# Seven block products for seven pairs of chunks of the first feed-forward layer too

## The chip, the cores and the metric

One core of a Trainium2 chip runs the whole program. The metric is the device time of one execution in microseconds; the kernel before has a median of 2299.14 us over three runs (2298.02 to 2299.99).

## The reference, cut to what matters

Two layers over 1024 tokens of width 1024, in float32. The first mixes tokens by gated linear attention and stick-breaking attention, the second by a convolution module; each is followed by a gated feed-forward layer (FFN) of width 2816.

```python
def swiglu(h, wg, wu, wd):
    return (jax.nn.silu(h @ wg) * (h @ wu)) @ wd

for layer in range(DEPTH):
    hn = rms_norm(h, mix_norm[layer])
    mix = hybrid_mixer(...) if layer % 2 == 0 else conformer_conv(...)
    h = h + mix
    h = h + swiglu(rms_norm(h, ffn_norm[layer]), ffn_w_gate[layer], ffn_w_up[layer], ffn_w_down[layer])
```

The convolution module is: a pointwise product to 2048 columns, a gate, a causal depthwise convolution of 31 taps, a layer norm over channels, swish, and a pointwise product back.

## The kernel before, in words

Every float32 operand is split into a rounded high part and the rest (`split`, `parts`), and each product takes three matmuls, high x high, high x low and low x high (`mm3`, lines 204 to 206). Residuals `xres` lie with tokens on partitions, 8 tiles of 128 tokens; activations for the products lie transposed, `hh_*`/`hl_*`, one pair for each half of 512 tokens. The 2816 columns of an FFN are 22 chunks of 128. `ffn_steps` builds for one half a step per chunk (gate, up, silu, product, split) and per group of chunks two down steps, each adding into `xres` (line 228). A step is a pair of functions, one that loads and splits weights and one that computes; `run` calls the first one step ahead. The weights' low parts are computed on the engine `weight_engine` names: VectorE in the first and last stage, GpSimd in the middle one. `raw_p` holds 2 raw weight tiles, `ws_p` 8 split ones.

A planner orders the instructions of each engine by program order and a simulated timeline, as far as dependences and free buffers allow; steps wrapped in `first` get priority by 2000 places. `behind` adds a dependence that only orders.

The stages: (1) attention. Near its end the attention of the second half (`a1`, `g1`, `o1`) is interleaved with all 22 FFN chunks of the first half (`f0`, groups of two). (2) The convolution stage: the output projection of the second half, then the pointwise chunks of the first half (`p0`) and the FFN of the second half (`f01`, groups of four) with the taps of the first half (`c0`, on VectorE, sums in PSUM) between; the layer norm `ln0`; then the second half's convolution (`c1`, two chunks of it on ScalarE and GpSimd) with the second FFN of the first half (`f10`, 11 chunks). `f10` stores the first of its two block products per matrix in DRAM (`m1_d`). (3) Five block products per matrix for the pairs of chunks f and f+11 of the second FFN: with the stored ones and the second one of `f10` these are seven block products (Winograd's form: 2 column blocks x 2 halves of the inner dimension x 2 halves of the tokens) in place of eight. Sums of token blocks (`token_sums`, `token_sum1`, `token_sum4`) overwrite the activations of both halves, sums of weight blocks are made in `pair_weights`, `pair_products` multiplies, `pair_down` adds the down products.

## Time and profile before

| | us |
|---|---|
| median of three runs | 2299.14 |
| the profiled execution | 2301.31 |
| its span, first to last instruction | 2299.5 |
| TensorE busy / VectorE / ScalarE / GpSimd | 2242.1 / 1591.4 / 959.5 / 473.9 |

The profile is of one execution. Busy times of TensorE (PE) overcount, since matmuls are pipelined: the distance between two starts is the better measure. PEld is TensorE's load of weights, DVE is VectorE, ACT ScalarE, POOL GpSimd. In the windows the clock is TensorE's granted clock as a share of its full one.

### The profile page before, as it was taken

To read this page: it belongs to the slowest core of one execution; us is meant where nothing else is said; L and a number is where in the kernel's file an instruction comes from. 1 tells how busy PE (TensorE), PEld (TensorE's weight loads), DVE (VectorE), ACT (ScalarE), POOL (GpSimd) and SP (SyncE) were. 2 spreads that over 40 slices of the span, in tenths; PEclk is the share of its full clock that TensorE was granted. 3 is DMA by queue.
4 is the path that set the end of the run, shared out by engine and by line. 5 is a ranking of instruction groups with operands and counts; after the bars stand their busy time and mean duration, and the time that the engine had idled before them with its cause. 6 is when DMAs were issued, how large, how long until landed. Compare 5 with 4: busy or idle time off the path is not lost.

```text
span 2299.5 us, 28002 instructions
## 1 busy us (share of the span) xinstructions
PE 2242.1 (98%) x10602; PEld 1855.6 (81%) x10602; DVE 1591.4 (69%) x2600; ACT 959.5 (42%) x1596; POOL 473.9 (21%) x255
## 2 busy tenths in 40 slices
PE   7999999999999999999999999999998899999999
PEld 6788888788888888888888887878886688888887
DVE  6587764878788755466677653897646677787776
ACT  6465544655565434423222254556345222222221
POOL 0000000000000004444444445979432000000000
PEclk9999999999999999999999999999999899999999
DMA  6254554223332334233222222233422222223222
GB/s 208 95 159 139 180 180 143 84 90 104 126 118 94 124 108 137 92 93 109 92 92 92 84 92 91 92 102 138 136 83 82 81 83 89 64 93 100 65 87 92
DMA packets 219637, 247.98 MB, mean 108 GB/s; under 512 B 9669, under 2 KB 169520, under 8 KB 219502
## 3 DMA queue, kind: packets, MB, share of 16 engines
q1 hardware_dynamic: 219502, 246.19, 33.1%
q8 instruction: 83, 1.36, 0.2%
q14 instruction: 52, 0.43, 0.1%
HBM read 219.42 MB, written 26.74 MB: 107 GB/s over the span
## 4 chain that ended last, share of the span: by engine, by line
PE 91%; DVE 4%; ACT 2%; DMA 1%; issue 1%; POOLq 0%; SPq 0%; POOL 0%; DVEq 0%; ACTq 0%
PE po L204 9%; PE po L205 9%; PE po L206 9%; PE pu L204 5%; PE pu L206 5%; PE pu L205 4%; PE pg L204 4%; PE pg L205 4%; PE pg L206 4%; PE pp L204 2%; PE pp L205 2%; PE pp L206 2%; PE po L674 2%; PE wt L656 1%; PE ps3u L204 1%
## 5 line engine op out<-in xcount | busy, mean ns | idle before, releaser
L941 DVE SCALAR_TENSOR_TENSOR cs<-u,wd,cs 128x512 f32<-128x512 f32 x406 | 306.2, 754 | 11.1
L228 DVE TENSOR_TENSOR xr<-xr,po 128x512 f32<-128x512 f32 x224 | 153.1, 684 | 157.7 <-PE po L206 156.7
L90 POOL TENSOR_TENSOR wl_wo<-raw_wo,wh_wo 128x1024 fp32r<-128x1024 f32 x8 | 19.1, 2398 | 883.4 <-ACT wh_wo L89 883.4
L1178 DVE TENSOR_TENSOR xr<-xr,po 128x512 f32<-128x512 f32 x176 | 120.1, 684 | 100.1 <-PE po L206 99.9
L204 PE MATMUL po<-wh_d,a 128*128 128x512 f32 x440 | 174.8, 399 | 6.9 <-ACT a L89 3.6
L204 PE MATMUL pg<-hh_f,wh_g 128*128 128x512 f32 x440 | 173.8, 395 | 5.5 <-DVE s L273 3.6
L206 PE MATMUL po<-wh_d,a 128*128 128x512 f32 x440 | 173.5, 395 | 4.1 <-DVE a L90 4.1
L205 PE MATMUL pg<-hl_f,wh_g 128*128 128x512 f32 x440 | 174.1, 396 | 0.0
L205 PE MATMUL po<-wl_d,a 128*128 128x512 f32 x440 | 173.7, 395 | 0.0
L206 PE MATMUL pg<-hh_f,wl_g 128*128 128x512 f32 x440 | 173.1, 394 | 0.0
L205 PE MATMUL pu<-hl_f,wh_u 128*128 128x512 f32 x440 | 172.7, 393 | 0.0
L204 PE MATMUL pu<-hh_f,wh_u 128*128 128x512 f32 x440 | 172.7, 393 | 0.0
L206 PE MATMUL pu<-hh_f,wl_u 128*128 128x512 f32 x440 | 172.6, 392 | 0.0
L89 ACT CAST wh_g<-raw_g 128x1024 fp32r<-128x1024 f32 x55 | 57.9, 1053 | 161.9 <-PE po L205 105.3
L90 POOL TENSOR_TENSOR wl_d<-raw_d,wh_d 128x1024 fp32r<-128x1024 f32 (+1 forms) x34 | 83.7, 2466 | 121.3 <-ACT wh_d L89 121.3
L90 POOL TENSOR_TENSOR wl_g<-raw_g,wh_g 128x1024 fp32r<-128x1024 f32 x33 | 79.3, 2404 | 135.6 <-ACT wh_g L89 131.6
L89 ACT CAST wh_d<-raw_d 128x1024 fp32r<-128x1024 f32 (+1 forms) x56 | 58.1, 1037 | 116.4 <-PE pu L205 66.8
L204 PEld LDWEIGHTS po<-wh_d,a 128*128 128x128 f32 x440 | 83.6, 190 | 25.6 <-DVE xr L228 4.7
L204 PE MATMUL po<-wh_dp,ap 128*128 128x512 f32 x264 | 102.0, 392 | 2.1 <-DVE xr L1178 1.0
L204 PE MATMUL pp<-hh_c,wh_p 128*128 128x512 f32 x256 | 100.0, 396 | 3.7 <-ACT hh_c L92 2.4
L204 PEld LDWEIGHTS pg<-hh_f,wh_g 128*128 128x128 f32 x440 | 83.5, 190 | 23.2 <-DVE s L273 3.8
L205 PE MATMUL pp<-hl_c,wh_p 128*128 128x512 f32 x256 | 101.7, 397 | 0.0
(440 smaller groups left out, 6067.6 us busy)
## 6 DMA issues: line engine op xcount, KB each, us to landing
raw_g<-in_ffn_w_gate_dram SPq DMA_DIRECT2D x27, 1024.0 KB, 5.2
raw_u<-in_ffn_w_up_dram SPq DMA_DIRECT2D x27, 1024.0 KB, 5.3
raw_p<-in_cv_w_pw_dram SPq DMA_DIRECT2D x16, 1024.0 KB, 5.4
raw_d<-in_ffn_w_down_dram SPq DMA_DIRECT2D x14, 1024.0 KB, 4.9
raw_d<-in_ffn_w_down_dram SPq DMA_DIRECT2D x24, 512.0 KB, 3.5
raw_g<-in_ffn_w_gate_dram SPq DMA_DIRECT2D x23, 512.0 KB
raw_u<-in_ffn_w_up_dram SPq DMA_DIRECT2D x23, 512.0 KB
raw_dp<-in_ffn_w_down_dram SPq DMA_DIRECT2D x22, 512.0 KB, 3.7
```

Source lines behind the costliest of these rows:

```text
L89: nc.scalar.copy(hi, src)
L90: (eng or nc.vector).tensor_sub(lo, src, r32(hi))
L204: nc.tensor.matmul(ps, sh, mh, start=first, stop=False, **kw)
L205: nc.tensor.matmul(ps, sh, ml, start=False, stop=False, **kw)
L206: nc.tensor.matmul(ps, sl, mh, start=False, stop=last, **kw)
L228: nc.vector.tensor_add(xt[i][:, cs], xt[i][:, cs], po)
L656: nc.tensor.transpose(pt[:, col:col + P], wrow[bi][:, P * j:P * j + P], ident)
L674: nc.tensor.matmul(po[:, lo_c:256], st["v"][j // 4][:, j % 4, e, :], m[:, 256 * jj + lo_c:256 * jj + 256], start=(last and jj == 0 and m i ...
L941: i = nc.vector.scalar_tensor_tensor(out, tap, w, acc, op0=ALU.mult, op1=ALU.add)
L1178: nc.vector.tensor_add(xres[i][:, cs], xres[i][:, cs], po)
```

## The change

The first FFN gets the same treatment as the second, for 14 of its 22 chunks: pairs f and f+7, f from 0 to 6. Chunks 14 to 21 stay plain.

- The first half's FFN beside the attention shrinks to chunks 0 to 6 (with stored first products) and 14 to 18.
- A new stage follows: chunks 19 to 21 of the first half, the output projection of the second half between, the token sums, the last two downs, then five block products for seven pairs.
- The convolution stage starts behind it. The FFN of the second half in it is chunks 14 to 21 alone. Chunks 1 and 4 of the first half's convolution run on ScalarE and GpSimd, as chunks 1 and 4 of the second half's did.
- The second FFN's order changes: chunk 10 runs ahead of the last pointwise products, groups are 3, 2, 3 and 3 chunks, and the token sums are one function for both layers. It keeps the first sum in PSUM, scales on two engines, makes the low parts of three sums on GpSimd and overwrites the first half's blocks at once. `token_sum4` also takes its low part from GpSimd and is put behind the last but one step.
- PSUM pools are given per tag, buffers `ft` 3 in place of 4 in the convolution stage and 10 in place of 6 in the last.

```diff
-    def ffn_steps(l, h, hT, xt, ps, ft, act, use_silu, group, last=NF, early=None):
+    def ffn_steps(l, h, hT, xt, ps, ft, act, use_silu, groups, keep=None):
...
-        f0 = ffn_steps(0, 0, lambda: hf, xres, ps, ft, act, False, 2)
+        f0 = ffn_steps(0, 0, lambda: hf, xres, ps, ft, act, False,
+                       [[0, 1], [2, 3], [4, 5], [6], [14, 15], [16, 17], [18]], m1_d[0])
...
-            + a1[:2] + [ffn_in] + interleave(f0[:-12], interleave(a1[2:], g1 + o1)) + f0[-12:])
+            + a1[:2] + [ffn_in] + interleave(f0[:-4], interleave(a1[2:], g1 + o1)) + f0[-4:])
...
+    def token_sums(l, hi_lo, ps, tags, ft, tiles, t3=None):
...
+        for j in range(2):
+            for i in range(4):
+                BOTH[i % 2](xn[i][j], xt[i][:, 512 * j:512 * j + 512], rs[:, i:i + 1])
+        for k in range(4):
...
+            nc.scalar.mul(r2, pt[1], g2)
+            nc.scalar.mul(b22[0][k], pt[1], g2)
+            sub1(r3, pt[0], g1, r2)
+            if t3 is not None:
+                split(b12[0][k], b12[1][k], pt[0], g1)
+            sub1(pt[0], pt[0], g1, r32(b11[0][k]))
+            nc.vector.tensor_sub(r1, pt[0], r32(b11[1][k]))
+            sub1(r2, pt[1], g2, r1)
+            split(t2[0][k], t2[1][k], r2, eng=nc.gpsimd)
+            sub1(b22[1][k], pt[1], g2, r32(b22[0][k]))
+            for t, r in ((t3 or b12, r3), (b11, r1)):
+                split(t[0][k], t[1][k], r, eng=nc.gpsimd)
+        return (b11, t2, t3 or b12, b21, b22), hi_lo[1]
+
+    def five_products(l, blocks, es, order):
...
+        before_t4 = marks[-2]
+
+        def token_sum4(k):
...
+            i = nc.vector.tensor_add(r, r32(t4[0][k]), r32(t4[1][k]))
+            behind(i.ins, before_t4)
...
+            split(t4[0][k], t4[1][k], r, eng=nc.gpsimd)
...
+            if l == 0 and f == NP - 1:
+                late = [pair_down(f, (0, 1), (h,)) for h in range(2)]
+            else:
+                late = [pair_down(f, (j,), (0, 1)) for j in range(2)]
+        return steps, late
...
+    with ExitStack() as mid:
+        weight_engine[0] = nc.vector
...
+            ps = psum_pools(es, "ps0", (("b", 2), ("a", 4), ("n", 2)))
...
+            f0 = ffn_steps(0, 0, lambda: hf, xres, ps, ft, act, True, [[19, 20, 21]])
+            load_x(1)
+            run(f0[:2] + out_project(1, ps, ft) + f0[2:3])
...
+            blocks, hT["f01"] = token_sums(0, hf, ps, ("n", "a"), ft, xn, [[t3[:, m, k, :] for k in range(4)] for m in range(2)])
+            run(f0[3:])
+        with ExitStack() as es:
+            steps, late = five_products(0, blocks, es, (("act", 4), ("s", 4), ("ft", 6), ("w", 2)))
+            run(steps + late)
...
-        f01 = ffn_steps(0, 1, lambda: hT["f01"], xres, ps, ft, act, True, 4)
-        f10 = ffn_steps(1, 0, lambda: hT["f10"], xres, ps, ft, act, True, 4, NP, m1_d)
-        c0 = conv_steps(0, range(NK))
+        f01 = ffn_steps(0, 1, lambda: hT["f01"], xres, ps, ft, act, True, [[14, 15, 16, 17], [18, 19, 20, 21]])
+        f10 = ffn_steps(1, 0, lambda: hT["f10"], xres, ps, ft, act, True,
+                        [[0, 1, 2], [3, 4], [5, 6, 7], [8, 9, 10]], m1_d[1])
+        c0 = interleave(conv_steps(0, (0, 2, 3, 5, 6, 7)), conv_steps(0, (1, 4), (1, 4)))
...
-        run([norm_step(0, mixg[1], "c0"), lambda: add_bias(0)] + p0[:2] + [norm_step(1, ffng[0], "f01")]
-            + interleave(p0[2:] + f01[:25], c0) + interleave(f01[25:31], ln0) + f01[31:]
-            + [norm_step(1, mixg[1], "c1"), lambda: add_bias(1)] + q0[:1] + p1[:2]
-            + interleave(q0[1:2] + p1[2:4] + q0[2:], c1[0])
-            + [norm_step(0, ffng[1], "f10")] + interleave(p1[4:] + f10[:9], c1[1])
-            + interleave(f10[9:13], ln1) + pw2(1, s1) + [token_sums] + f10[13:15] + [token_sum1] + f10[15:])
...
+        run([norm_step(0, mixg[1], "c0"), lambda: add_bias(0)] + f01[:2] + p0[:2]
+            + interleave(p0[2:] + f01[2:9], c0) + interleave(f01[9:], ln0)
+            + [norm_step(1, mixg[1], "c1"), lambda: add_bias(1)] + q0[:2] + p1[:2]
+            + interleave(p1[2:4] + q0[2:], c1[0])
+            + [norm_step(0, ffng[1], "f10")] + interleave(p1[4:] + f10[:12], c1[1])
+            + interleave(f10[12:14] + f10[16:17], ln1) + pw2(1, s1))
+        xn = [t for pair in u_pairs("xn_f11") for t in pair]
+        blocks, _ = token_sums(1, hT["f10"], ps, ("n", "a"), ft, xn)
+        run(f10[14:16] + f10[17:])
```

## Rows read from the trace of the kernel before

**Rows 1.** Part 1 of the page: busy time and share of each engine.
```profile
PE 2242.1 (98%) x10602; PEld 1855.6 (81%) x10602; DVE 1591.4 (69%) x2600; ACT 959.5 (42%) x1596; POOL 473.9 (21%) x255
```
**Rows 2.** Timeline of TensorE, last stage: start, duration, instruction.
```profile
1817.72 0.39 PE L205 MATMUL ps2g<-hl_f,wh_s3ag 128*128 128x512 f32 x1
...
1819.98 0.39 PE L206 MATMUL ps1u<-t,wl_s24u 128*128 128x512 f32 x1
```
**Rows 3.** Windows: busy us (instructions) of PE, PEld, DVE, ACT, POOL; clock, DMA.
```profile
430.00:800.00 370.00, 366.14 (x1883) 306.71 (x1882) 294.18 (x444) 198.81 (x377) 0.00 (x0) 1.00 0.33 104
...
960.00:1310.00 350.00, 350.00 (x1561) 289.72 (x1560) 237.01 (x328) 94.19 (x113) 154.71 (x77) 1.00 0.30 97
...
1394.00:1435.00 41.00, 37.27 (x171) 29.85 (x170) 14.45 (x30) 21.19 (x36) 20.07 (x14) 0.96 0.15 55
1435.00:1650.00 215.00, 211.15 (x943) 174.25 (x942) 179.55 (x249) 114.56 (x169) 167.26 (x103) 0.99 0.34 112
...
1741.00:1811.30 70.30, 50.55 (x201) 39.10 (x199) 55.89 (x89) 30.41 (x49) 16.53 (x6) 0.81 0.28 86
1811.30:2299.50 488.20, 482.30 (x2112) 394.72 (x2112) 357.43 (x517) 112.84 (x150) 0.00 (x0) 1.00 0.26 84
```
**Rows 4.** Timeline of TensorE, transition of the second FFN.
```profile
1760.79 1.03 PE L1032 MATMUL pt_f<-ident,xn_f 128*128 128x128 f32 x8
...
1773.11 0.63 PE L205 MATMUL pg<-hl_f,wh_g 128*128 128x512 f32 x1
1773.54 0.63 PE L206 MATMUL pg<-hh_f,wl_g 128*128 128x512 f32 x1
```
**Rows 5.** Groups of VectorE instructions, 430 to 800 us: busy, mean ns, idle before.
```profile
L228 DVE TENSOR_TENSOR xr<-xr,po 128x512 f32<-128x512 f32 x56 | 38.1, 681 | 13.0 <-PE po L206 12.9
L90 DVE TENSOR_TENSOR wl_u<-raw_u,wh_u 128x1024 fp32r<-128x1024 f32 x17 | 20.7, 1219 | 0.8 <-ACT wh_u L89 0.8
...
L273 DVE TENSOR_TENSOR s<-s,pg 128x512 f32<-128x512 f32 x18 | 12.3, 681 | 0.1
```
**Rows 6.** Timeline of VectorE, transition of the second FFN.
```profile
1740.98 0.69 DVE L228 TENSOR_TENSOR xr<-xr,po 128x512 f32<-128x512 f32 x1 [2.03 <-PE po L206]
...
1748.59 0.16 DVE L112 SCALAR_TENSOR_TENSOR rs_f<-nt_f,rs_f 128x4 f32<-128x4 f32 x1
...
1753.68 0.75 DVE L1039 SCALAR_TENSOR_TENSOR r<-pt_f,vb,hh_f 128x512 f32<-128x512 f32 x1 [1.37 <-PE pt_f L1032]
...
1762.82 0.74 DVE L1041 SCALAR_TENSOR_TENSOR r<-pt_f,vb,r 128x512 f32<-128x512 f32 x1
1763.48 0.74 DVE L93 SCALAR_TENSOR_TENSOR hl_f<-pt_f,vb,hh_f 128x512 fp32r<-128x512 f32 x1
...
1793.81 1.27 DVE L228 TENSOR_TENSOR xr<-xr,po 128x512 f32<-128x512 f32 x2
```
**Rows 7.** Groups of GpSimd instructions, 1441 to 1606 us.
```profile
L935 POOL TENSOR_TENSOR cv<-cv,tap 128x512 f32<-128x512 f32 x60 | 77.8, 1296 | 7.2 <-ACT tap L934 4.7
L90 POOL TENSOR_TENSOR wl_p<-raw_p,wh_p 128x1024 fp32r<-128x1024 f32 x11 | 26.5, 2405 | 9.9 <-ACT wh_p L89 9.9
```
**Rows 8.** Timeline of VectorE, convolution of the first half.
```profile
1086.30 4.71 DVE L941 SCALAR_TENSOR_TENSOR cs<-u,wd,cs 128x512 f32<-128x512 f32 x6
```
**Rows 9.** Timeline of VectorE, layer norm statistics of one tile.
```profile
1347.90 1.29 DVE L961 BATCH_NORM_STATS2 bst<-plt 128x6 f32<-128x512 f32 x2 [5.54 <-PE plt L960]
...
1353.97 0.16 DVE L965 SCALAR_TENSOR_TENSOR lv<-lv 128x1 f32<-128x1 f32 x1
```
**Rows 10.** Timeline of GpSimd (POOL) and VectorE (DVE), the same transition.
```profile
1743.69 2.40 POOL L90 TENSOR_TENSOR wl_u<-raw_u,wh_u 128x1024 fp32r<-128x1024 f32 x1
1743.79 2.32 DVE L105 TENSOR_SCALAR nv_f<-s_f 128x4 f32<-128x4 f32 x1
...
1778.53 6.29 POOL L90 TENSOR_TENSOR wl_d<-raw_d,wh_d 128x1024 fp32r<-128x1024 f32 x1 [19.85 <-ACT wh_d L89]
1783.13 2.23 DVE L1110 TENSOR_TENSOR raw_g<-s1g,raw_g 128x512 f32<-128x512 f32 x1
```

More of the change, by code (lines that the diff above doesn't have):

```diff
@@ L26 @@
 NF = DFF // P
-NP = NF // 2
+NPS = (7, NF // 2)
 EPS = 1e-6
@@ L251, in chunk @@
                 pr.append(ps.tile([P, 512], F32, name=f"p{t}{nm}", tag="a"))
-                if early is None:
+                if not kept:
                     for k in range(NK):
@@ L255, in chunk @@
                             k == 0, k == NK - 1)
-            if early is not None:
+            if kept:
                 for k0 in (0, 4):
@@ L330, in trunk @@
     o_d = dr("o_d", [8, P, T])
-    m1_d = dr("m1_d", [2, NP, P, TH])
+    m1_d = [dr(f"m1_d{l}", [2, NPS[l], P, TH]) for l in range(2)]
     xres = [None] * NT
@@ L1084, in token_sum4 @@
-        def token_sum4(k):
-            r = ft(f"t4_{k}")
-            nc.vector.tensor_add(r, r32(t4[0][k]), r32(t4[1][k]))
-            nc.vector.tensor_sub(r, r, r32(t2[0][k]))
-            nc.vector.tensor_sub(r, r, r32(t2[1][k]))
-            split(t4[0][k], t4[1][k], r)
-        def product(pm, w, b, first=True, alone=False):
-            for k in range(4):
-                mm3(pm, w[0][:, k, :], w[1][:, k, :], b[0][k], b[1][k], first and k == 0, k == 3,
-                    skip_group_check=not alone)
```

304 lines of the change are left out of this document (151 added, 153 removed).

## The prediction, made before the changed kernel was run

> **What bounds the kernel now.** I read the page's busy times first: TensorE is busy 98% of the span, VectorE 69% [rows 1]. Since matmuls overlap, busy is not the measure; the start-to-start pitch is. In the last stage ten pitches of 512 columns take 2.26 us, so one costs 0.2267 us [rows 2]. The table by stage comes next [rows 3]: 430 to 800 us (first FFN of the first half, with the attention of the second half), 960 to 1310 (first FFN of the second half with the convolution of the first) and the last stage keep TensorE at 99 to 100%. Work taken from TensorE is therefore time, as long as nothing else comes late in its place. One stretch is different: from the last residual add that the second half's norm needs, at 1741.0 us, to the first of the five block products at 1811.3 us. It holds 169 matmuls of 512 columns and 32 transposes (201 in all), 169 x 0.227 + 32 x 0.11 (8 transposes take 1.03 us end to end [rows 4]) = 41.8 us of work at the full clock, in 70.3 us: 28.5 us are lost there (granted clock 0.81; after an idle spell the pitch is 0.43 us, the 1.2 GHz level [rows 4]). VectorE is busy 55.9 of the 70.3 us. This stretch is the model for the new one that the change builds in the first FFN.
>
> **What is removed.** Seven pairs of chunks, gate and up each, take seven block products in place of eight. A block product is 4 x 3 = 12 matmuls, so 7 x 2 x 12 = 168 matmuls go: 168 x 0.2267 = **38.1 us** of TensorE. Transposes (32 for the norm of the second half) and the down products keep their number. This is the only gain that is certain; all else is where TensorE will wait.
>
> **Attention of the second half (430 to 800).** The filler shrinks from 18 chunks and 14 downs of two chunks to 12 chunks, 8 such downs and 2 of one chunk. TensorE loses 6 x 48 + 120 = 408 matmuls = 92 us of the 370; 277 are left. VectorE loses per chunk two weight splits of 1.22 and three passes of 0.68 (4.5 us, x 6 = 27), and 16 adds of 0.68 and 7 weight splits of 1.22 (19 us) [rows 5]: 294 - 46 = 248 us [rows 3]. It would be 89% full, against 80% now with 3.9 us of TensorE idle, and against 84% with 3.9 us idle in 1435 to 1650 [rows 3]. I take **+3 us** (bounds 0 and 15). The copies and stores of the kept first products (14 of each) lie on ScalarE, busy 199 of 370 us, and on the DMA engines, busy a third [rows 3]; nothing.
>
> **New stage, its token sums.** T0 is the last add of the output projection of the second half. Today's case shows the chain behind such an add: the root is done 7.8 us later, the first token sum starts after 12.7 us [rows 6]. The change splits the scaling between two engines; I take 10.5. On VectorE then stand 24 passes (6 per k) at a pitch of 0.66 = 15.8, 16 adds of the last two downs at 0.60 = 9.6 [rows 6], product and split of chunk 21, 1.2, one down weight split 1.2 and one of the first pair's weights, 1.2: 29 us. At a fill of 85% (80% in today's stretch [rows 3]) that is 34 us: the first product starts at T0 + 44.6. TensorE has from T0 on chunk 21 and the two downs, 48 + 72 matmuls, and 32 transposes: 30.7 us. Lost: 14 us. The fourth token sum then must be there within four products (10.9 us): 12 passes, 7.2 us, and its GpSimd halves take 1.3 us each [rows 7]. Its first pass is pinned behind the last but one down; product five waits for it, and the sums for the up matrix's weights stand behind it in VectorE's queue: +2. **+16 us**, bounds: 0, if TensorE finds filler as it does in nearly all of 960 to 1310, and 28.5, today's whole loss.
>
> **The same stretch in the second FFN** is rebuilt. Chunk 10 moves ahead, so that the halves can be overwritten at once, and the cover is four downs of 36 matmuls and 32 transposes, 36.2 us. VectorE: 20 passes 13.2, 28 adds 16.8, weight sums 2.4, one split 1.2: 33.6, at 85% 39.5 us, so T0 + 50: 14 lost. The fourth sum is pinned in the same way, and its GpSimd halves (4 x 1.3) compete with down weights of 2.4 us: +5. 19 in place of 28.5: **-10 us** (bounds -25 and +5).
>
> **Convolution stage.** 14 of 22 chunks of the second half leave it, and with them 228 us of cover; out-projection and one norm leave too. Chunks 1 and 4 of the first half's convolution go to ScalarE and GpSimd. VectorE keeps 6 x 31 = 186 taps. They depend on one another: six take 4.71 us, 0.785 each [rows 8], 146 us; some 34 other passes between them cost about 0.5 each where they fill that latency: 17. From its start TensorE has 6 pointwise and 6 FFN chunks and 4 downs of 48 matmuls, 768 x 0.2267 = 174 us, and 64 transposes, 7. The convolution ends at 163; behind it four layer norm statistics of some 4 us (6.2 in the row, 2.2 of it blocked [rows 9]) and half the swish, 22 us in all: 185 against 181. Then +4, and +2 for queueing; the second norm behind it gets two downs as cover in place of one and returns the 3.7 us idle of 1394 to 1435 [rows 3]. **+2 us** (bounds -5 and 30). GpSimd carries 60 adds of 1.30 and weight splits of 2.40 [rows 7], some 150 us in these 163; in 1435 to 1650 it was busy 167 of 215 with TensorE idle 3.9 [rows 3]. The second half's convolution has the same taps and about the same cover: **+1** (bounds -4 and 8). The second layer norm keeps 3 chunks as cover and loses a down of 48 matmuls, 10.9 us: **+3** (0 and 11).
>
> **Stage changes.** Attention to the new stage: 38 us of cover (four downs, two chunks) where 87 stood. Five products to convolution: the last pair's halves are ordered so that 48 matmuls of downs and two chunks (33 us) lie over the norm, but the last activation is not covered. **+4** (0 and 10). DMA and SP's queue: 14 more stores and loads of 256 KB, and the loads of x moved ahead, at a DMA share of a quarter to a third [rows 3]; nothing. Five products in steady state ran 488 us with 5.9 idle [rows 3], most of it at the end of the kernel; 7 pairs the same: nothing.
>
> **A rule against the change.** The first token sums and all of the fourth put 16 splits on GpSimd. Today a VectorE pass over 4 columns takes 2.32 us while GpSimd runs a split (others of the kind 0.16 [rows 6]), a GpSimd split takes 6.29 in place of 2.40 beside VectorE's passes, and a VectorE pass 2.23 behind it [rows 10]. The Trainium skill (SBUF — State Buffer, "Who interferes with whom") states that a VectorE instruction with two SBUF inputs and a GpSimd instruction that reads SBUF exclude each other for a whole instruction; the trace agrees with these rows. By that rule the token sums, with one input in PSUM, run free, but the fourth one does not; with it the sum is the third rival's, without it the +2 and +5 above stand.
>
> **Sum.** -38.1 + 3 + 16 - 10 + 2 + 1 + 3 + 4 = -19.1 us. The profiled execution took 2301.3 us (span 2299.5 and 1.8 around it): 2282.2. The median of the runs, 2299.14, lies 2.2 below it: **2280**.
>
> **Rivals.**
> 1. Less is lost: the planner finds filler, and the new stretch costs no more than a us or two, as 960 to 1310 shows for a well filled stage. -19.1 - 14.3 = -33: 2266. Against it: VectorE's queue of 29 us stands whatever TensorE does.
> 2. No change: the new stretch costs today's full 28.5 us and the old one stays. -38.1 + 3 + 28.5 + 2 + 1 + 3 + 4 = +3.4: 2302.5. For it: the same dependences, and less cover than today (30.7 against 41.8 us).
> 3. Slower, by the shared port: each of the four GpSimd splits of the fourth sum takes 6.29 in place of 2.40, and product five waits: 4 x 3.9 = 15.6 at each of both places, -19.1 + 31.2 = +12: 2311. It decides once one such split delays TensorE by more than 2.4 us. Against it: the other products and adds from PSUM open gaps.
> 4. Slower, by the convolution: TensorE doesn't run ahead, so it follows VectorE (163 against 141 us up to the last FFN chunk of that stage, 22) and then has too little cover for the statistics (13 more): 35 in place of 2 on that term, 2313. It decides once TensorE idles over 21 us more in that stage. Against it: today the passes of the FFN slip between the taps.
> That the change doesn't do what it says would show as more than 10,434 matmuls, and I give it nothing.
>
> **Chances.** Forecast 0.54 (own range 2262 to 2294), rival 1 0.13, rival 2 0.12, rival 3 0.11, rival 4 0.10. A measurement can tell about 0.2% (4.6 us) from no change: faster 0.67, same 0.12, slower 0.21. The range reaches from below rival 1 to just short of rival 3: 2258 to 2310.
>
> **What would show it.** About 10,434 TensorE instructions on the page (records can be missing); a stretch between the last add of the output projection and the first block product of the first FFN with some 16 us lost and the clock below 1; the second such stretch shorter than 70 us; VectorE near 90% beside the attention of the second half and in the convolution of the first; GpSimd splits well over 1.3 us in the stretches (rival 3). I am wrong if the new stretch loses under 5 or over 25 us, or if TensorE idles over 10 us in the convolution of the first half.

## The result, and the profile after

The changed kernel takes **2387.9 us** in the median of 4 runs (2386.95 to 2388.62) beside 2299.56 of the kernel before on the same chip: **1.0383 times** as long, 95% interval 1.0365 to 1.0401. Forecast were 2280, range 2258 to 2310. The profiled execution has a span of 2385.2 us; the clock granted over the whole of it is 0.97.

The page's first part, busy time and share of each engine, against [rows 1]:

```profile
PE 2240.0 (94%) x10434; PEld 1843.5 (77%) x10434; DVE 1697.1 (71%) x2784; ACT 1003.7 (42%) x1684; POOL 476.5 (20%) x299
```

The 168 matmuls are gone (10602 to 10434). TensorE's busy time is nearly what it was, 2240 against 2242, although 38 us of work went: a matmul takes longer where the granted clock is low, and that is 0.97 over the span where it was 0.99. VectorE is busy 106 us more. The windows of the changed kernel, in the columns of [rows 3], cut at events (last output of an attention unit 763.5; last add of the output projection 836.6; first block product 887.9; statistics of the norm ahead of the convolution 1224.8; first chunk of pointwise products through 1257.6; first layer norm statistics 1447.5; then the second half's convolution, layer norm and token sums):

```profile
430.00:763.50 333.50, 308.91 (x1554) 255.71 (x1552) 266.96 (x416) 186.37 (x369) 0.00 (x0) 0.95 0.35 112
763.50:836.60 73.10, 72.49 (x317) 59.45 (x318) 31.91 (x40) 26.41 (x41) 0.00 (x0) 1.00 0.29 95
836.60:887.90 51.30, 25.74 (x124) 20.02 (x123) 49.05 (x81) 25.06 (x41) 20.96 (x14) 0.81 0.24 72
887.90:1224.80 336.90, 327.71 (x1425) 267.40 (x1426) 225.48 (x325) 83.85 (x119) 20.93 (x13) 0.99 0.26 83
1224.80:1257.60 32.80, 29.46 (x131) 23.34 (x131) 11.18 (x28) 16.13 (x23) 14.50 (x11) 0.92 0.11 35
1257.60:1447.50 189.90, 182.34 (x798) 149.82 (x797) 162.56 (x224) 87.25 (x117) 160.67 (x103) 0.99 0.31 100
1447.50:1487.70 40.20, 21.98 (x93) 17.87 (x94) 20.79 (x85) 20.60 (x40) 0.50 (x3) 0.60 0.04 13
...
1580.40:1758.60 178.20, 173.78 (x775) 142.90 (x774) 142.59 (x200) 90.07 (x129) 124.80 (x76) 0.98 0.37 118
1758.60:1809.70 51.10, 39.30 (x182) 32.01 (x181) 25.72 (x82) 24.22 (x37) 11.51 (x5) 0.83 0.26 91
...
1844.00:1893.80 49.80, 35.88 (x174) 29.36 (x172) 41.44 (x75) 21.63 (x37) 29.18 (x19) 0.92 0.22 69
1893.80:2382.10 488.30, 484.91 (x2112) 396.08 (x2112) 364.23 (x520) 115.70 (x153) 6.72 (x4) 0.99 0.27 86
```

As in the prediction, **lost** is the elapsed time less TensorE's work in it (0.2267 us for each matmul of 512 columns, fewer columns in proportion, 0.11 for a transpose). It holds idle time and the low clock together. Between the same events of both kernels:

| stretch | lost before | lost after | more | forecast |
|---|---|---|---|---|
| up to 430 us | 43.5 | 43.1 | -0.4 | 0 |
| 430 to the last attention unit | 12.8 | 50.8 | +38.0 | +3 |
| output projection | (stage changes) 2.1 | 1.2 | -0.9 | |
| first FFN's token sums, to the first product | - | 27.2 | +27.2 | +16 |
| five products of the first FFN, norm ahead of the convolution | - | 22.3 | +22.3 | +4 |
| first half's convolution and layer norm | 0.5 | 35.8 | +35.3 | +2 |
| up to the second half's layer norm | 12.5 | 11.7 | -0.8 | +1 |
| second half's layer norm | 2.6 | 16.9 | +14.3 | +3 |
| second FFN's token sums | 28.9 | 14.5 | -14.4 | -10 |
| last stage | 6.3 | 9.6 | +3.3 | 0 |

The last stage is counted up to its last add to the residual, some 3 us ahead of the span's end in both kernels. The sum of "more" is +123.9 us; less the 38.1 saved it is +85.8, the difference of the two spans (2385.2 - 2299.5 = 85.7).

What such a stretch looks like: TensorE's timeline at the first half's layer norm; in brackets the idle time ahead of an instruction and what ended it.

```profile
1446.21 0.47 PE L1161 MATMUL plt<-ident,cv 128*128 128x128 f32 x1 [6.19 <-DVE cv L1142]
1451.04 1.97 PE L1161 MATMUL plt<-ident,cv 128*128 128x128 f32 x8 [4.35 <-ACT lx L1168]
1457.41 1.97 PE L1161 MATMUL plt<-ident,cv 128*128 128x128 f32 x8 [4.41 <-ACT lx L1168]
1463.86 1.97 PE L1161 MATMUL plt<-ident,cv 128*128 128x128 f32 x8 [4.49 <-ACT lx L1168]
1470.31 1.97 PE L1175 MATMUL pls<-ident,lx 128*128 128x128 f32 x8 [4.48 <-ACT lx L1168]
```

The four tiles of statistics follow one another 6.4 us apart with nothing between them, and eight transposes take 1.97 us where they took 1.03 [rows 4]: the granted clock is 0.60 there. The chain is that of [rows 9]; before, the chunks of the first FFN lay over it.

### The profile page after: what moved, and what is told of

Same layout as the page of the kernel before. It is cut to its first block, busy times and chain, and to the rows that moved or that the text cites. A ratio compares the mean times of both kernels' runs of the same rounds, so it can differ in the third digit from the quotient of the medians.

```text
span 2385.2 us, 28069 instructions
## 1 busy us (share of the span) xinstructions
PE 2240.0 (94%) x10434; PEld 1843.5 (77%) x10434; DVE 1697.1 (71%) x2784; ACT 1003.7 (42%) x1684; POOL 476.5 (20%) x299
## 4 chain that ended last, share of the span: by engine, by line
PE 83%; DVE 10%; ACT 2%; DMA 2%; issue 1%; SPq 0%; DVEq 0%; ACTq 0%
PE po L205 8%; PE po L206 8%; PE po L207 8%; PE pg L205 3%; PE pg L207 3%; PE pg L206 2%; PE pu L205 2%; PE pu L207 2%; PE pu L206 2%; PE pp L205 2%; PE pp L206 2%; PE pp L207 2%; PE ps3u L205 1%; PE ps3u L206 1%; PE ps2u L207 1%; PE ps2u L206 1%
## 5 line engine op out<-in xcount | busy, mean ns | idle before, releaser
L205 PE MATMUL po<-wh_dp,ap 128*128 128x512 f32 x432 | 167.1, 392 | 3.8 <-DVE xr L1015 2.1
L207 PE MATMUL po<-wh_dp,ap 128*128 128x512 f32 x432 | 165.3, 390 | 0.9 <-DVE ap L91 0.9
L206 PE MATMUL po<-wl_dp,ap 128*128 128x512 f32 x432 | 165.9, 389 | 0.0
L1136 POOL TENSOR_TENSOR cv<-cv,tap 128x512 f32<-128x512 f32 x120 | 155.6, 1296 | 11.2 <-ACT tap L1135 4.9
L205 PE MATMUL po<-wh_d,a 128*128 128x512 f32 x272 | 109.1, 402 | 7.8 <-DVE xr L229 7.8
L205 PE MATMUL pg<-hh_f,wh_g 128*128 128x512 f32 x272 | 107.7, 397 | 5.5 <-DVE s L277 4.6
L207 PE MATMUL po<-wh_d,a 128*128 128x512 f32 x272 | 107.8, 398 | 0.2 <-DVE a L91 0.2
L206 PE MATMUL pg<-hl_f,wh_g 128*128 128x512 f32 x272 | 107.6, 395 | 0.0
L206 PE MATMUL po<-wl_d,a 128*128 128x512 f32 x272 | 107.2, 394 | 0.0
L207 PE MATMUL pu<-hh_f,wl_u 128*128 128x512 f32 x272 | 107.1, 394 | 0.0
L207 PE MATMUL pg<-hh_f,wl_g 128*128 128x512 f32 x272 | 106.9, 393 | 0.0
L1135 ACT ACTIVATE tap<-u,wd 128x512 f32<-128x512 f32 x120 | 84.6, 720 | 50.9 <-POOL cv L1136 50.8
```

Of the source, the lines that this page charges most:

```text
L205: nc.tensor.matmul(ps, sh, mh, start=first, stop=False, **kw)
L206: nc.tensor.matmul(ps, sh, ml, start=False, stop=False, **kw)
L207: nc.tensor.matmul(ps, sl, mh, start=False, stop=last, **kw)
L1135: nc.scalar.mul(m, tap, w)
L1136: nc.gpsimd.tensor_add(acc, acc, m)
```

## The experiments

The theory at the start: TensorE's chunks, moved out of the attention and convolution stages, had been cover for the chains of other engines. Rivals: GpSimd's splits hold VectorE up; the second FFN's rebuild is the cause; the work is there but TensorE's planned order puts it in the wrong place; another engine's total work sets a stage's length.

### Which part of the change: l1_only, l0_only

Edit of l1_only (layer 0 and the convolution of the first half as before):

```diff
-        f0 = ffn_steps(0, 0, ..., [[0, 1], [2, 3], [4, 5], [6], [14, 15], [16, 17], [18]], m1_d[0])
+        f0 = ffn_steps(0, 0, ..., [[f, f + 1] for f in range(0, NF, 2)])
...
-    with ExitStack() as mid:
...
```

> The second FFN's part of the change alone (its token sums, its order of chunks, its fourth sum pinned); the first FFN and the first half's convolution as before. Cover theory (TensorE's other work, moved out of the attention and convolution stages of the first FFN, leaves chains bare there): the stretch in front of the second FFN's products loses some 14 us in place of 28.7, the second layer norm some 8 to 16 in place of 2.7, so 2286 to 2300 us, faster than before or the same. If the loss of the changed kernel sat mainly in the second FFN's rebuild, this would be slower than before by over 30 us. Port theory (GpSimd's splits of the token sums hold VectorE up): the stretch in front of the products does not shrink, 28 us or more lost, and the time is 2300 or above.

Edit of l0_only: the second FFN's token sums, its order and its last stage are the ones of before.

```diff
-        blocks, _ = token_sums(1, hT["f10"], ps, ("n", "a"), ft, xn)
-        run(f10[14:16] + f10[17:])
+            + interleave(f10[9:13], ln1) + pw2(1, s1) + [token_sums] + f10[13:15] + [token_sum1] + f10[15:])
```

> The first FFN's part alone (seven pairs, the stage of its own, convolution behind it with two chunks on ScalarE and GpSimd); the second FFN as before. Cover theory: attention tail 36 us lost, token sums 27, norm ahead of the convolution 15, first layer norm 33, against 38 saved: 2385 to 2400 us, the whole of the loss and a little more, since the second FFN's transition again loses about 28. If the two parts disturb one another, this is well below 2380.

Measured: l1_only 2304.1 us, ratio 1.0019 (1.0010 to 1.0028); l0_only 2387.5, ratio 1.0384 (1.0369 to 1.0400). The first FFN's part carries the whole loss. The second FFN's part is worth nothing, as a sum of large terms: the stretch of its token sums loses 12.5 us in place of 28.9, but the layer norm ahead of it 15.7 in place of 2.6 and the last stage 12.5 in place of 6.3. The stretches of l1_only: convolution and layer norm of the second half, token sums, last stage:

```profile
1498.80:1675.50 176.70, 172.82 (x773) 141.89 (x772) 133.33 (x188) 87.30 (x125) 120.88 (x73) 0.99 0.38 120
1675.50:1725.40 49.90, 38.09 (x182) 31.16 (x181) 25.71 (x82) 24.12 (x37) 11.54 (x5) 0.86 0.28 92
1759.70:1807.40 47.70, 38.55 (x173) 30.04 (x172) 43.12 (x69) 20.80 (x34) 27.73 (x18) 0.96 0.31 95
1807.40:2298.70 491.30, 484.68 (x2113) 395.50 (x2111) 366.77 (x526) 116.77 (x155) 7.38 (x4) 1.00 0.26 83
```

### The size of the shift: np4, att_cover, att_less

```diff
# np4 (of the lists of chunks, the ends of the lines)
-NPS = (7, NF // 2)
+NPS = (4, NF // 2)
-[[0, 1], [2, 3], [4, 5], [6], [14, 15], [16, 17], [18]], m1_d[0])
+[[0, 1], [2, 3], [8, 9], [10, 11], [12, 13], [14, 15], [16, 17], [18]], m1_d[0])
-[[14, 15, 16, 17], [18, 19, 20, 21]])
+[[8, 9, 10, 11], [12, 13, 14, 15], [16, 17, 18, 19], [20, 21]])
# att_cover (the end of a line, and the stage behind)
-[16, 17], [18]], m1_d[0])
+[16, 17], [18, 19], [20]], m1_d[0])
-            f0 = ffn_steps(0, 0, lambda: hf, xres, ps, ft, act, True, [[19, 20, 21]])
+            f0 = ffn_steps(0, 0, lambda: hf, xres, ps, ft, act, True, [[21]])
...
# att_less (the end of a line)
-[[0, 1], [2, 3], [4, 5], [6], [14, 15], [16, 17], [18]], m1_d[0])
+[[0, 1], [2, 3], [4, 5], [6]], m1_d[0])
```

> Four pairs in place of seven: TensorE saves 21.8 us in place of 38.1, three more chunks and their downs (49 us of work) lie beside the attention, six more chunks (98 us with their downs) beside the convolution. Cover theory: the attention tail loses under 10 us in place of 36, the first layer norm under 10 in place of 33, the token sums and the norm ahead of the convolution still 27 and 15: 38.1 - 21.8 - 28 - 25 = -37, some 2350 us, less if the norms find more cover. Theory that the pairs themselves or their stores and loads cost time, pair by pair: 88 us x 4/7 = 50 above before, also near 2350; they part in where it goes: by the second the attention stage and the layer norm keep more than half their losses. Theory that it is the new stage as such (its barriers and transitions, whatever the number of pairs): the saving falls and the loss stays, 2404 us.

> Chunks 19 and 20 and their downs, 144 matmuls or 33 us of work, go from the new stage into the attention stage; nothing else is changed. Cover theory with a tail that only lacks cover: the attention stage ends at the same time (763 us) with 33 us of work more in it, its tail loses 36 - 33 = 3 to 8 us; the token sums lose as much more as they lose cover (two downs of one chunk in place of three: 11 us) and the output projection loses the two chunks beside it: net -10 to -22, some 2365 to 2378. Cover as a zero-sum game between the two places: no change, 2388. If the attention's tail is slow for another reason (VectorE full, GpSimd, DMA), its end moves back by the 33 us of added work and the time rises, 2395 or more.

> The changed kernel without chunks 14 to 18 of the first half and their downs (360 matmuls, 81.6 us of TensorE's work, left out); VectorE loses some 45 of its 266 us with them, ScalarE some 15. Floor theory (the attention's own chain takes some 330 us whatever lies beside it, as att_hold's 328 suggests): the attention ends at 755 to 764 as before, and of the 81.6 us nearly all is lost: 2365 to 2378. VectorE theory: 221 us of work at the same 80% fill take 276, the stage ends near 710, 2325 to 2340. TensorE theory (units at the tail's bare pace of 12 us as soon as nothing lies beside them): it ends near 680, below 2310.

Measured: np4 2340.1 us, ratio 1.0176 (1.0159 to 1.0193); att_cover 2391.7, ratio 1.0402 (1.0387 to 1.0418); att_less 2348.7 in one run.

With four pairs the convolution and its layer norm lose 1.1 us in place of 35.8: there the work was cover, and enough of it covers all. The token sums (27.6) and the norm ahead of the convolution (21.3) lose with four pairs what they lose with seven. The stretches of np4: attention, token sums, convolution, layer norm:

```profile
430.00:785.40 355.40, 344.04 (x1772) 287.84 (x1770) 288.45 (x441) 195.90 (x377) 0.00 (x0) 0.99 0.36 112
860.40:912.10 51.70, 25.98 (x124) 19.92 (x123) 49.02 (x82) 24.98 (x41) 20.92 (x14) 0.80 0.24 71
1150.30:1364.40 214.10, 214.10 (x950) 177.16 (x949) 166.41 (x229) 95.48 (x128) 170.23 (x108) 1.00 0.30 98
1364.40:1428.50 64.10, 63.48 (x309) 52.84 (x307) 37.28 (x91) 30.65 (x44) 28.63 (x12) 1.00 0.27 95
```

The attention stage still loses 23.5, though 49 us of work came back to it; in att_cover, with 35 us more work, it ends 22 us later. So its tail does not simply lack work. (What att_cover won there, 13 us, the output projection and the token sums lost again, which had given up the work.) These are the attention stages of before, after and the kernels that differ in its work, from 430 us to the last unit:

| kernel | TensorE's work, us | length, us | VectorE busy, us | its fill (busy share) |
|---|---|---|---|---|
| before | 356 | 369.2 | 294 | 80% |
| att_cover | 318 | 355.6 | 284.7 | 80% |
| np4 | 332 | 355.4 | 288.5 | 81% |
| after | 283 | 333.5 | 267.0 | 80% |
| att_less | 202 | 297.8 | 229.4 | 77% |

From before to after 73.7 us of work go and the stage gets 35.7 us shorter; from after to att_less 80.7 go and it gets 35.7 shorter: each us taken from TensorE gave 0.48 and 0.44 us. With it went 27 and 38 us of VectorE's work, so these runs do not tell the two engines apart. VectorE was never over 81% full, before included, where TensorE bounded the stage. In att_less, TensorE's waits from 560 to 728 us are for the units' own passes (engine, tile and line that waits, and for what; total us, times, longest):

```profile
PE po L676 <- DVE og L683: 12.0, 4, 3.1
PE po L676 <- ACT wth L90: 11.5, 6, 2.6
PE wt L658 <- ACT c L312: 7.3, 11, 1.2
```

### What sets the attention stage: att_pool, att_hold, att_nosplit

```diff
# att_pool: around the weights of each first-FFN step of the attention stage
+                weight_engine[0] = nc.gpsimd
+                ws = step[0]()
+                weight_engine[0] = nc.vector
# att_hold: matmuls of a step of f0 stand behind the attention unit written ahead of it
+                        for i in mine:
+                            behind(i, last[0])
# att_nosplit: in parts(), for the same steps
+        if no_split:
+            nc.scalar.copy(hi, raw_ap)
+            return hi, hi
```

> In the attention stage GpSimd (idle there) takes the lower-half weight splits of the first FFN's chunks and downs, 15 x 2 of 1.2 us and 16 of 0.7 to 1.2, some 50 us of VectorE's 266. Theory that VectorE bounds the attention's bare tail (busy 62 of the 73 us): the attention stage ends 10 to 25 us earlier than 763.5 and its 50.8 us lost fall to 26 to 40. Cover theory pure (each unit's chain of sigmoid, scan, transposes and splits takes its 11 us, TensorE's other work is gone by 690): the tail starts with the last chunk, whichever engine splits its weights; the end moves by under 5 us. Port theory: VectorE's passes next to GpSimd's splits stretch, the stage gets longer.

> The changed kernel, but TensorE may start each step of the first FFN (a chunk or a down) in the attention stage only behind the attention unit that is written ahead of it; in the changed kernel the last of this work is done at 690 us and the last six of sixteen units run bare. Order theory: the work lasts to the end of the attention, the units ahead of 690 come earlier and the last ones have cover: of 50.8 us lost in the stage 15 to 30 come back, 2357 to 2372. Chain theory (the units can't come faster than now even with TensorE free for them, their scans, sigmoids and splits take turns): the losses move from the tail into the time before 690, and the stage takes 330 to 345 us as before, 2385 to 2395.

> The changed kernel, whose first-FFN steps in the attention stage leave out the lower half of their weights' split (the upper half stands for both): VectorE loses 30 passes of 1.22 us and some 14 of 0.7 to 1.2, about 48 of its 266 us; TensorE has every matmul, and GpSimd nothing more. VectorE theory (its work, 80% of the stage and 85% of the tail, sets the end of the attention): the stage ends 20 to 40 us before 763.5 and loses 15 to 30 in place of 50.8, 2350 to 2368. Chain theory (one unit's sigmoid, scan, product, transposes and splits follow one another, and their waits, not their work, take the time): the end stays within 8 us, 2380 to 2388.

Measured, one run each: att_pool 2385.5 us, att_hold 2407.1, att_nosplit 2378.5; the stage takes 335.6, 328.4 and 322.1 us against 333.5. The windows of att_pool, att_hold and att_nosplit:

```profile
430.00:765.60 335.60, 309.27 (x1561) 253.97 (x1559) 270.18 (x382) 186.05 (x369) 88.72 (x35) 0.96 0.37 114
```
```profile
430.00:758.40 328.40, 292.75 (x1459) 240.85 (x1458) 252.56 (x390) 181.59 (x362) 0.00 (x0) 0.92 0.30 94
```
```profile
430.00:752.10 322.10, 302.49 (x1559) 252.01 (x1557) 234.43 (x382) 185.10 (x369) 0.00 (x0) 0.97 0.36 112
```

att_hold speaks against the order: with the work held back, 67 us are lost in the stage, most of it ahead of 690 us. Its tenth unit of sixteen ends 36 us earlier than in the changed kernel, but the last one 5 us earlier. att_nosplit takes 32.5 us from VectorE, and the stage ends 11.4 earlier, 0.35 for one: VectorE's work is a part of what sets the length, not all of it. (It also leaves the tiles of the lower halves free, so that not even the 0.35 is VectorE's for certain.) att_pool could not tell, since VectorE stayed as busy (270 us in 34 passes fewer). Its pass b<-b,c over 1023 columns, after and att_pool, 430 to 763 us (columns as in [rows 5]):

```profile
L648 DVE TENSOR_TENSOR b<-b,c 128x1023 f32<-128x1023 f32 x7 | 8.5, 1216 | 0.0
```
```profile
L648 DVE TENSOR_TENSOR b<-b,c 128x1023 f32<-128x1023 f32 x7 | 15.5, 2213 | 0.1
```

What the rest is (a unit's own sequence of sigmoid, scan, product, transposes and splits is the candidate that att_less's waits name) was not tried by itself and stays open.

### The token sums: t1_bufs, t1_dve, t1_pin

```diff
# t1_bufs
-            ftp = es.enter_context(tc.tile_pool(name="ft0", bufs=3))
+            ftp = es.enter_context(tc.tile_pool(name="ft0", bufs=6))
# t1_dve
-            split(t2[0][k], t2[1][k], r2, eng=nc.gpsimd)
+            split(t2[0][k], t2[1][k], r2, eng=(nc.vector, nc.gpsimd)[l])
...
# t1_pin, on top of t1_bufs (and the up matrix's first two passes alike)
-            behind(i.ins, before_t4)
+            behind(i.ins, ts_last[l])
```

> The new stage's scratch tiles for the token sums (ft0): six buffers in place of three. Buffer theory: ScalarE's copy for round k waits until GpSimd has split the tile of two rounds before, which makes rounds of 9 us; with six buffers the stretch from the last add of the output projection to the first product shrinks from 51.3 us to some 35 to 42, and 27 us lost become 11 to 18, time near 2375. Queue theory (VectorE's order of work sets the rounds) and port theory (GpSimd's splits slow VectorE): 51 us stay, 2388.

> In the first FFN's token sums and fourth sum, the 16 lower-half splits go from GpSimd to VectorE; buffers as in the changed kernel. Port theory (a GpSimd split and a VectorE pass with two SBUF inputs exclude each other, as VectorE passes of 1.6 to 1.75 us in place of 0.6 beside such splits suggest): VectorE's passes fall back to 0.6 us, the stretch shrinks by 10 us or more from 51.3. Queue theory: VectorE gets 12 more passes of 0.6 us before the last second-sum tile, 7 us: the stretch grows to 55 to 60. Buffer theory: tiles come free as soon as VectorE is through, so it shrinks a little, 45 to 50.

> Six buffers as in t1_bufs, and besides VectorE's passes that the first product doesn't need (the 12 passes of the fourth sum and the first two passes of the up matrix's sums) may not run before the last token sum, in both FFNs. In t1_bufs VectorE has no gap from 847 to 886 us and runs some 12 passes of the fourth sum and 4 passes of the up matrix's sums, 13 us, ahead of the last second-sum tile. Queue theory: the stretch falls from 44.0 to 32 to 37 us, lost 8 to 13, time 2370 to 2376; product five then waits for the fourth sum by 0 to 5 us of it. If the chain of rounds (transpose, ScalarE, VectorE, GpSimd) sets the pace whatever stands in VectorE's queue, 44 stay, 2382. In the second FFN's stretch (49.8 us, 14.5 lost) the same holds with the same sign.

Measured, one run each: 2381.8, 2384.8 and 2383.8 us; the stretch 44.0, 54.5 and 36.5 us against 51.3. **Buffers**: in the changed kernel GpSimd splits r2 of an earlier round from 868.61 to 870.85, and ScalarE, which waits 3.34 us for that, starts its copy into the tile at 870.89. With six buffers the stretch is 7.3 us shorter.

```profile
870.89 0.69 ACT L883 ACTIVATE r<-pt_f,vb 128x512 f32<-128x512 f32 x1 [3.34 <-POOL t L91]
```

**Port**: without GpSimd's splits the passes with two SBUF inputs are short again (three of the four t<-t,t had taken 1.57 to 1.75 us), but the stretch gets 3 us longer, since VectorE now has the splits too. So this run does not price the slow passes by themselves. The group t<-t,t of after and of t1_dve, 836 to 889 us:

```profile
L917 DVE TENSOR_TENSOR t<-t,t 128x512 f32<-128x512 f32 x4 | 5.7, 1434 | 0.0
```
```profile
L917 DVE TENSOR_TENSOR t<-t,t 128x512 f32<-128x512 f32 x3 | 2.0, 680 | 0.0
```

**Queue**: in t1_bufs VectorE has no gap from 858 to 882 us, and in it stand passes that the first product doesn't need: fourth sum (L915 to L918) and sums of the up matrix (L937 on):

```profile
861.36 2.48 DVE L915 TENSOR_TENSOR t<-hh_f,hl_f 128x512 f32<-128x512 f32 x4
863.77 0.68 DVE L937 TENSOR_TENSOR s1u<-raw_u 128x512 f32<-128x512 f32 x1
864.37 0.74 DVE L882 SCALAR_TENSOR_TENSOR r<-pt_f,vb,r 128x512 f32<-128x512 f32 x1
865.03 0.67 DVE L938 TENSOR_TENSOR raw_g<-raw_g 128x512 f32<-128x512 f32 x1
865.63 0.68 DVE L917 TENSOR_TENSOR t<-t,t 128x512 f32<-128x512 f32 x1
```

Put behind the last token sum (t1_pin), they let the first product start 7.5 us earlier, as forecast; then they are late for the products behind it, which lose 25.7 in place of 16.6. TensorE's waits of t1_pin, 876 to 960 us:

```profile
PE ps1g L205 <- ACT t L90: 10.8, 1, 10.8
PE ps3g L205 <- DVE vg L963: 7.5, 1, 7.5
```

The add vg stands in VectorE's queue behind the passes moved. The four passes just ahead of it have two SBUF inputs, run beside GpSimd's splits and take 6.7 us in place of 2.7, so 4 us of this wait come with the splits. So of the 27 us some 7 are buffers; the rest goes with VectorE's queue, whose work comes before the first product or right behind it.

### The norm ahead of the convolution: c0_pin, c0_wd

```diff
# c0_pin: the first two chunks of f01
+                behind(next(i for i in nc.cur_bb.bb.instructions[n:] if i.engine == mybir.EngineType.PE), last_down0)
# c0_wd: the load and transposes of the convolution's weights as a step
-            + f01[:2] + p0[:2]
+            + f01[:2] + p0[:1] + [conv_weights] + p0[1:2]
```

> Only TensorE's order at the end of the new stage is changed: the two chunks (96 matmuls, 21.8 us) that were written behind the norm ahead of the convolution may not run before the first half's last downs are done. Cover theory: they then lie over the norm's chain; the 15.2 us lost up to the norm's statistics and the 7.1 behind them fall by 10 to 18 in all, time 2370 to 2378. If the chunks were run early because TensorE had nothing else there (waiting for the last pair's activation), the loss only moves ahead, to the time before the downs, and 2388 stays.

> The changed kernel with one block moved: loading the convolution's weights and transposing them (8 small transposes) comes behind the first pointwise chunk of the convolution stage in place of ahead of its norm. In the changed kernel TensorE waits 4.5 and 2.2 us in its queue for these two loads, at 1221 and 1224 us, in the 22.3 us lost around that norm. DMA theory: the wait is part of the path and goes, 2379 to 2382. Norm theory: the norm's chain (squares, root, scaling, from 1217 on) takes the wait's place, and the first norm transposes still come at 1232, 2385 to 2389.

Measured, one run each: 2391.7 and 2383.2 us. Held chunks recover nothing: 27.1 us are lost in place of 22.3. Without the wait for the weights' loads TensorE waits for ScalarE's s of a chunk instead; of after and of c0_wd, around 1195 to 1264 us:

```profile
PE pwd L1080 <- DMA wdrow<-in_cv_w_dw_dram: 6.7, 2, 4.5
```
```profile
PE pu L205 <- ACT s L273: 6.3, 1, 6.3
```

20.6 us are lost in place of 22.3. The wait was there, but another stood right behind it: in ScalarE's queue this s comes behind the eight passes of squares of the norm (1216.51 to 1221.51 in c0_wd). What would be lost with s ahead of them was not tried.

### The convolution and the layer norms: ln0_pace, ln0_taps, ln0_pin, l1_fix, l1_pin

```diff
# ln0_pace
-            + interleave(p0[2:] + f01[2:9], c0) + interleave(f01[9:], ln0)
+            + interleave(p0[2:] + f01[2:6], c0) + interleave(f01[6:], ln0)
# ln0_taps
+                    if h == 0 and 16 <= j < 24:
+                        continue
# ln0_pin (in_order puts the matmuls of a step behind those of the step before it in the list)
+            + interleave(p0[2:] + f01[2:8], c0)
+            + in_order([ln0[0], f01[8], ln0[1], f01[9], ln0[2], f01[10], ln0[3], f01[11]] + ln0[4:], never)
# l1_fix, on l1_only
-            + interleave(p1[4:] + f10[:12], c1[1]) + interleave(f10[12:14] + f10[16:17], ln1)
+            + interleave(p1[4:] + f10[:9], c1[1]) + interleave(f10[9:14] + f10[16:17], ln1)
# l1_pin, on l1_only
+            + interleave(p1[4:] + f10[:11], c1[1])
+            + in_order([ln1[0], f10[11], ln1[1], f10[12], ln1[2], f10[13], ln1[3], f10[16]] + ln1[4:], never) + pw2(1, s1))
```

> Only the order written for TensorE in the convolution stage is changed: three steps of the first FFN (a chunk and two downs or two chunks and a down, 33 us of TensorE work) move from beside the convolution to beside the layer norm of the first half. Pacing theory (each convolution piece stands behind a step of TensorE's list, so that every step written beside the convolution makes it longer, and none is left for the layer norm): the convolution ends up to 20 us earlier, the layer norm loses 5 to 12 us in place of 26, time 2368 to 2376. Bound theory (VectorE at 90% and GpSimd at 90% set the convolution's end, as the second half of the losses' table reads): the convolution's stretch loses what the layer norm gains, its loss goes from 10 to 25 to 35, and the time stays within 5 us of 2388.

> The first half's convolution leaves out taps 16 to 23 of 31, 48 dependent passes of VectorE (some 37 us) and 16 on ScalarE and GpSimd; all else as in the changed kernel. Bound theory (VectorE and GpSimd carry the convolution and set its end; TensorE's chunks run out beside it): the convolution ends 25 to 37 us earlier than 1445, the layer norm then has chunks beside it, and of the 10 and 26 us lost there 25 to 36 come back: 2350 to 2362. If the layer norm lies bare for the planner's order alone (TensorE's chunks are placed ahead of it whenever the convolution ends), TensorE idles in its chain as before: the 26 us of the layer norm stay, and only the convolution's 10 come back, 2375 to 2380.

> The changed kernel with TensorE's order at the first half's layer norm written by hand: the last two chunks and the last two downs (192 matmuls, 43.5 us) between and behind the tiles of statistics. Order theory: of the 25.7 us lost in the layer norm 15 to 20 come back, and the convolution, which has 33 to 44 us less beside it, ends up to 10 us earlier and loses up to 15 more: net -5 to -15, 2372 to 2382. Bound theory (VectorE's whole work of convolution, chunks and layer norm sets the end): the layer norm gains what the convolution loses, 2385 to 2392.

> As l1_only (the second FFN's part alone), but three of the steps written beside the second half's convolution (a chunk and two downs, or so, 33 us) go beside its layer norm. In l1_only the stretch in front of the products lost 12.5 in place of 28.9, and the layer norm 15.7 in place of 2.6, so that nothing was won. Pacing theory: the convolution ends at about 1652 again as before, the layer norm loses 2 to 6, the stretch ahead of the products still 12 to 15: 2286 to 2293, faster than before. If cover is a zero-sum game here too, 2300 to 2304.

> As l1_only and l1_fix (the second FFN's part alone), with TensorE's order at the second half's layer norm written out by hand: transposes of one tile's statistics, then a whole chunk of the FFN (48 matmuls, 10.9 us), four times, then the rest. In l1_fix 52 us of TensorE's work lay in that stretch and 14.2 us were lost all the same, in two gaps of 4.5 us and at the low clock behind them. Order theory (the work is there, but the planner's list, made with durations that are not the chip's, places it ahead of the chain and not between the tiles): the layer norm loses 1 to 5 us, the stretch in front of the products still 12, time 2287 to 2293, faster than before. Chain theory (VectorE or ScalarE hold the tiles up whatever TensorE does between them): each chunk waits for its own passes too, 10 to 16 lost as before, 2300.

The convolution's length runs, in the first half, from the end of the first chunk of pointwise products to the first layer norm statistics, in the second half from the norm's statistics ahead of it.

| kernel | us | lost beside the convolution | lost in the layer norm | convolution's length |
|---|---|---|---|---|
| after (first half) | 2387.9 | 10.1 | 25.7 | 189.9 |
| ln0_pace | 2392.4 | 20.0 | 25.1 | 182.0 |
| ln0_pin | 2403.6 | 43.3 | 6.1 | 180.3 |
| ln0_taps | 2371.8 | 1.7 | 18.5 | 161.4 |
| before (second half) | 2299.6 | 6.1 | 2.6 | 151.9 |
| l1_only | 2304.1 | 6.6 | 15.7 | 176.7 |
| l1_fix | 2300.8, ratio 1.0006 (0.9996 to 1.0015) | 6.1 | 14.2 | 150.8 |
| l1_pin | 2300.3, ratio 1.0002 (0.9993 to 1.0012) | 15.1 | 4.3 | 160.3 |

Work that is moved from the convolution to the layer norm covers the layer norm when its place is written by hand (ln0_pin, l1_pin), and is then missing beside the convolution. The two stretches of ln0_pin:

```profile
1261.50:1441.80 180.30, 139.94 (x610) 115.02 (x609) 155.55 (x213) 77.19 (x105) 141.43 (x95) 0.88 0.26 82
1441.80:1503.90 62.10, 60.19 (x278) 48.59 (x277) 28.83 (x88) 30.26 (x52) 19.55 (x11) 0.96 0.23 77
```

With 43 us less of TensorE's work the convolution is 10 us shorter, and VectorE is busy 155.6 of 180.3 us, 86%, as in after (162.6 of 189.9). With 48 of VectorE's 186 dependent taps left out (ln0_taps) the loss beside the convolution is gone, VectorE is 75% full (121.7 of 161.4) and the total is 16 us shorter:

```profile
1259.30:1420.70 161.40, 161.40 (x710) 133.22 (x709) 121.70 (x168) 72.61 (x97) 129.19 (x83) 0.99 0.31 102
```

ln0_taps also leaves out 16 of GpSimd's 60 adds, and GpSimd was as busy as VectorE (160.67 of 189.9), so the run alone does not tell which of the two sets the end. The trace of the changed kernel does: GpSimd's last add ends at 1422.98 us, VectorE's last tap at 1446.16, and TensorE's statistics wait for that tap. The same order holds in ln0_pin, ln0_pace and ln0_taps. VectorE's idle time has names too: 13.3 of its 27.3 us are waits for the sigmoids of the pointwise products, 8.1 of them ahead of the first tap (the last two lines are read as the waits of att_less):

```profile
1420.31 2.67 POOL L1136 TENSOR_TENSOR cv<-cv,tap 128x512 f32<-128x512 f32 x2
1445.41 0.75 DVE L1142 SCALAR_TENSOR_TENSOR cv<-u,wd,cs 128x512 f32<-128x512 f32 x1
DVE u L1111 <- ACT sg L1110: 13.3, 7, 8.1
DVE pu L279 <- PE pu L207: 5.0, 6, 1.1
```

So VectorE's queue sets the convolution's end. In the second half, work moved from one place to the other was worth about the same; in the first half it was worth more beside the convolution (ln0_pin loses 49.4 us in both stretches together, after 35.8). In ln0_pace and l1_fix moving the work in the written order alone changed little in the layer norm: in l1_fix the planner left two gaps of 4.5 us between the tiles all the same, in ln0_pace it filled none and ran 16 us of downs behind the statistics.

## Why the prediction was wrong

**Matmuls, -38.1**: right, 168 fewer, and the sum of the losses closes with that. (The ten pitches of 2.26 us make 0.226 us each, not 0.2267; that is 0.1 us on this term.)

**Attention, +3, bounds 0 and 15; measured +38.** The step that failed is "89% full", taken as reachable. Every kernel run stayed at 77 to 81% of VectorE there, apart from att_nosplit (73%); at 80% the forecast 248 us of VectorE's work would have been 310, and it was 267, so 333. The second size was the work that goes: 92 us in the forecast, 74 up to the last unit, since a part of the old filler had lain behind it. The 80% of [rows 3] was read as room that VectorE would use once TensorE had less to do; with TensorE's work taken away it stayed at 80%. What holds it there is not shown: att_nosplit's 73% speaks against a fixed ceiling.

**Token sums, +16, bounds 0 and 28.5; measured +27.2**, inside its bounds and over the 25 that the prediction named as a sign of being wrong. Two sizes were off. The stretch took 51.3 us in place of 44.6: eleven of the twelve passes of the fourth sum and the sums of the up matrix stood in VectorE's queue (busy 49.05), which the forecast had left behind the first product, and ft0's three buffers cost 7 (t1_bufs). And TensorE had 24.1 us of work in it in place of 30.7, since 29 matmuls of chunk 21 had run ahead of the last add. With six buffers, what is lost before and behind the first product is 36 to 38 us together whichever way the queue is written (t1_bufs 19.9 and 16.6, t1_pin 12.4 and 25.7).

**Second FFN's token sums, -10; measured -14.4**: right in mechanism and size. But the cover came out of the layer norm ahead (+14.3 for a forecast of +3, bounds 0 and 11), so the second FFN's part is worth nothing (l1_only, l1_fix, l1_pin: 1.0019, 1.0006, 1.0002).

**Convolution of the first half, +2, bounds -5 and 30; measured +35.3.** The step that failed is the end of the convolution: VectorE's work was forecast at 163 us and is 162.6, and the end was put at 163 as if nothing else held it up; it took 189.9, with the waits named above. The statistics and swish behind it were put at 22 us with 4 for a tile, "2.2 of it blocked"; bare, the tiles came 6.4 apart and the stretch took 40.2. This is rival 4, which named the place and put 35 in place of 2: TensorE follows VectorE and has too little left for the statistics. Its two parts, 22 and 13, came out as 10.1 and 25.7 (TensorE idle for 7.6 and 18.2 us), so the place was right and the close match of the sum luck. **Stage changes, +4, bounds 0 and 10; measured +22.3**, with the products of the first FFN ahead of it, which had been put at nothing: neither chunks held back nor the loads taken away recover it, and its cause beyond the waits seen in c0_wd stays open.

**Rival 3**, the shared port: VectorE's passes between SBUF operands did take 1.43 us in place of 0.68 beside GpSimd's splits, which agrees with the rule of the Trainium skill (SBUF — State Buffer, "Who interferes with whom") named in the prediction. Of the rows given there, the pass over 4 columns has one SBUF input, so that it is no case of the rule as the prediction puts it. The size did not come: the longest of these splits took 2.26 us in the first FFN's stretch and 3.96 in the second's, not 6.29 each. What remains of it is not priced (t1_dve has the stretch 3 us longer and the whole 3 us shorter without them, in one run). **Rival 1** and **rival 2** fall with the sum.

What the prediction had wrong as a whole: each stage's loss was bounded by the loss seen in a well filled stage, or by the one bare transition. Where the filler is taken away, the stage ends when its other chains end: VectorE's taps in the convolution, and in the attention something of which VectorE's work is a part.

## What to carry to other kernels

Before work is taken from a saturated engine, work out for each stage that loses some the time that its other engines need by themselves: as a first estimate, the busy time of the next engine over the fill that it has now, not over 100%. It fits the attention of four kernels here (80 to 81%) and not att_nosplit, so look also for the waits that make its gaps. Work removed below that floor returned half (attention) or a quarter (ln0_pin's convolution, 10 us for 43), and the granted clock fell in the gaps. Moving cover from one bare chain to another won nothing in any try here: l1_fix and l1_pin end level with the kernel before, ln0_pace, att_cover and ln0_pin 4, 4 and 16 us behind the changed one.

## What the runs showed of the hardware

- A bare stretch costs more than its idle time. In the attention's tail, from 690 to 763.5 us, 36.4 us are lost and TensorE is idle for 18.5 of them; it is busy 54.99 us for 37.1 us of work. The granted clock is 0.81, so the clock can account for at most 14 us (0.19 of 73.5), a good third of the loss.

```profile
690.00:763.50 73.50, 54.99 (x263) 44.64 (x261) 62.49 (x100) 37.95 (x82) 0.00 (x0) 0.81 0.24 76
```

- VectorE's pass of 1023 columns with both inputs in SBUF took 2213 ns on average with GpSimd's weight splits beside it and 1216 without (att_pool), while its adds from PSUM kept their 0.68 us. Handing 34 of VectorE's passes to an idle GpSimd (35 splits of 2.53 us) left VectorE's busy time where it was, 270 against 267 us.
